# Summing the squares for a norm from a token-major copy of x, and moving the first key projection ahead of it

## The chip, the cores and the metric

The kernel runs on one core of a Trainium2 chip, as one program. The metric is device time in microseconds (us) of one execution. The time of a kernel is the median of its runs. Beside the timed runs there is one execution with the hardware profiler on, and all rows of a trace come from that one.

The core has five engines that work side by side and wait for one another through semaphores: PE (matrix products; PEld is its weight load), DVE (vector operations), ACT (functions, scaled copies), POOL (slower vector work) and SP (which here only issues DMA transfers). Each engine runs its instructions strictly in the order in which they stand.

## The reference, cut to what matters

One step of a hybrid decoder layer: 512 prompt tokens and 8 x 4 sample tokens, 544 rows of 1024 numbers, go through an RMS norm, one wide projection (75 tiles of 128 columns), three token mixers, a merge and an output projection. The change touches only the beginning:

```python
def rmsnorm(x, g):
    xf = x.astype(jnp.float32)
    y = xf * lax.rsqrt(jnp.mean(xf * xf, axis=-1, keepdims=True) + EPS)
    return (y * g.astype(jnp.float32)).astype(x.dtype)
...
parts = split_cols(rmsnorm(x, lp['norm_g']) @ lp['w_in'])
q = rmsnorm(parts['a_q'].reshape(B, T, A_HEADS, A_HD), lp['a_qn']) * (A_HD ** -0.5)
kv = parts['a_kv'].reshape(B, T, 3, 2, A_KV, A_HD)
```

## The kernel before, in words

x is held transposed: `xT` has the 1024 features on 128 partitions in 8 pieces, and the 544 tokens along each row. Every product is made in three parts of reduced-precision operands: a weight tile is split into a rounded part `wh` (ACT, L396) and a rest `wl` (DVE or POOL, L399), the activations into `uh` (ACT, L446) and `ul` (DVE, L449), and PE adds wh·uh, wh·ul and wl·uh over the 8 pieces. One tile is 2 halves of 272 tokens x 24 products (L410, in `gemm_steps`); a half goes into one of two PSUM buffers `pj`, and a sink empties it.

The norm is not applied before the first projections. `uh` and `ul` hold x times the norm's gain only; the factor of each token, 1/sqrt(mean square), is multiplied in when a half is emptied: the sinks at L746 (queries and keys), L755 (values) and L500 (the gate tile) multiply by `rb`, a tile in which the factor of every token stands in all 128 partitions. `rb` is the "row" in question. Nothing that passes through a sink can leave PSUM before `rb` is there.

How `rb` is made before: x is squared piece by piece (POOL L443, ACT L444), pairs of pieces are added (DVE L447), and PE sums over the partitions by products with a column of ones (L453, 4 groups of 5 products, each of which PE runs in two passes, so that the trace counts 10). DVE scales the sums (L460, L461), POOL raises them to -0.5 (L463), PE spreads the 5 columns over all partitions (L468, 10 in the trace), and ACT (L469) and DVE (L470) copy them to `rb`. The sums are interleaved with the 48 products of the first tile (`misc`, the gates; L458), and 13 products of zeros (L438) run ahead of it all. Then come six key and value tiles and four query tiles, on `uh` and `ul`, each with its weight split, its sinks, and for keys and queries a square on ACT (L747) and sums on PE (L742). In the same stretch DVE makes the normalized x for the later tiles (`norm`, L475, L478) and a long series of small gate computations (L609 to L700).

The program is written in one sequence; a scheduler of the framework orders it per engine by its own estimate of times and by priorities. The loads of all weight tiles are issued by SP, in order, into three buffers `wr`; a load waits until the `wl` of the tile three before has been made. Every DMA also waits for the one issued eight before it from SP and ACT together.

Of the kernel before, what the change touches and what calls it, by code (L numbers as in the profile page):

```python
# [19 lines left out]
D = 1024  # L20
T = 512
# [18 lines left out]
NWARM = 13  # L40
# [132 lines left out]
def _layout(i):  # L173
# [4 lines left out]
    d['xT'] = x.T.reshape(8, 128, N).transpose(1, 0, 2)  # L178
    cols = np.array(_col_order())
# [67 lines left out]
def tile_step(ctx: ExitStack, tc: tile.TileContext, A, O):  # L247
# [117 lines left out]
    sqr_ = BS.ring(5, N)  # L365
# [68 lines left out]
    nc.sync.dma_start(out=cst[:, 128:], in_=A['cst'][:, 128:])  # L434
# [4 lines left out]
    pss = pat()  # L439
    pm = [pat()[:, :HF] for h in range(2)]  # L440
    for k in range(0, 8, 2):
        s0, s1 = sqr_(), sqr_()
        nc.gpsimd.tensor_tensor(out=s1, in0=xT[:, k + 1, :], in1=xT[:, k + 1, :], op=ALU.mult)  # L443
        nc.scalar.activation(out=s0, in_=xT[:, k, :], func=AF.Square)  # L444
        for i in (k, k + 1):
            nc.scalar.activation(out=uh[:, i, :], in_=xT[:, i, :], func=AF.Copy, scale=V(VG + i))  # L446
        nc.vector.tensor_tensor(out=s1, in0=s1, in1=s0, op=ALU.add)  # L447
        for i in (k, k + 1):
            nc.vector.scalar_tensor_tensor(out=ul[:, i, :], in0=xT[:, i, :], scalar=V(VG + i), in1=uh[:, i, :].bitcast(F32),  # L449
                                           op0=ALU.mult, op1=ALU.subtract)  # L450
        for i in (0, 1, 2, 4, 3):
            r = 128 if i < 4 else NS
            nc.tensor.matmul(pss[:r, i:i + 1], lhsT=s1[:, i * 128:i * 128 + r], rhs=ones, start=(k == 0 and i == 0),  # L453
                             stop=(k == 6 and i == 3))
        for c in (k, k + 1):
            for j, (w, m) in enumerate(((wt0[0], uh), (wt0[1], uh), (wt0[0], ul))):
                for h in range(2):
                    nc.tensor.matmul(pm[h], lhsT=w[:, c, :], rhs=m[:, c, h * HF:h * HF + HF], start=(c == 0 and j == 0),  # L458
                                     stop=(c == 7 and j == 2))
    nc.vector.tensor_scalar(out=ss[:, :4], in0=pss[:, :4], scalar1=1.0 / D, scalar2=EPS, op0=ALU.mult, op1=ALU.add)  # L460
    nc.vector.tensor_scalar(out=ss[:NS, 4:5], in0=pss[:NS, 4:5], scalar1=1.0 / D, scalar2=EPS, op0=ALU.mult, op1=ALU.add)  # L461
# [7 lines left out]
    nc.scalar.copy(out=rb[:, :T], in_=pb)  # L469
    nc.vector.tensor_copy(out=rb[:, T:], in_=pb2[:, :NS])  # L470
# [17 lines left out]
    nc.vector.tensor_copy(out=ptf, in_=pti)  # L488
    for q in range(NQ):
        nc.vector.tensor_scalar(out=idxf[:, :, q], in0=ptf, scalar1=float(8 * NQ), scalar2=C('pm8'), op0=ALU.mult, op1=ALU.add)  # L490
        nc.vector.tensor_scalar(out=idxf[:, :, q], in0=idxf[:, :, q], scalar1=float(q), scalar2=None, op0=ALU.add)
    nc.vector.tensor_copy(out=idxi, in_=idxf)
# [258 lines left out]
    for b in range(3):  # L751
        rw = rwr()
        raw.append(rw)
        proj(J_KV + 2 * b, qk_sink(b, rw, sqr()))
        proj(J_KV + 2 * b + 1, lambda s, p, b=b: nc.vector.tensor_tensor(out=vTt[b][:, s], in0=p, in1=rb[:, s], op=ALU.mult))  # L755
        with low(400):
            norm(2 * b)
            norm(2 * b + 1)
        nc.scalar.dma_start(out=O['kv'][2 * b + 1], in_=vTt[b])
# [93 lines left out]
    for src, d in ((RBt.rearrange("p b r -> p (b r)"), rb2), (V(VREL, 8), vr2)):  # L853
        nc.scalar.copy(out=d[:, 0, :], in_=src)
        nc.vector.tensor_tensor(out=d[:, 1, :], in0=src, in1=d[:, 0, :].bitcast(F32), op=ALU.subtract)
# [1157 lines left out]
```

## Time and profile before

| | us |
|---|---|
| median of 3 runs | 987.78 |
| lowest and highest of the runs | 981.44, 989.70 |
| the profiled execution | 992.92 |
| its span, first to last instruction | 990.7 |
| PE busy in the span | 940.4 |
| DVE busy in the span | 507.8 |
| ACT, POOL busy in the span | 359.1, 310.0 |

The span is the time from the first to the last instruction; 2.2 us of the profiled execution lie around it. A busy PE is not a PE at its peak: a product counts as busy whether PE's clock is granted at full (2.4 GHz, shown as 1.00) or at half (1.2 GHz, shown as 0.50). Over the span the granted clock is 0.971 on average. Shares over the whole span say little about a change in the first 100 us; the rows that count are those of that stretch.

### The profile page before, as it was taken

The numbers are of one execution on the slowest core, as the hardware profiler recorded it, in microseconds if no ns is written. First come the engines' busy times: TensorE is split into PE (matmuls) and PEld (weight loads), VectorE is DVE, ScalarE is ACT, GpSimd is POOL, SyncE is SP. The second block draws the span as 40 slices with busy tenths as digits, with TensorE's granted clock in tenths as the row PEclk, the third lists the DMA queues.
The fourth block names the chain that finished last, engine by engine and source line by source line (L and its number), as shares of the span: only waits on it lengthen the run. The fifth ranks groups of instructions, "written<-read, shape, count | busy, mean of one in ns | idle before, by whom it ended". The sixth has DMA issues, their size and how long they took to land.

```text
span 990.7 us, 21616 instructions
## 1 busy us (share of the span) xinstructions
PE 940.4 (95%) x8609; PEld 854.9 (86%) x8609; DVE 507.8 (51%) x1256; ACT 359.1 (36%) x728; POOL 310.0 (31%) x369
## 2 busy tenths in 40 slices
PE   8999899799999999999999979999999899999998
PEld 7888798786789977789998959999989777899998
DVE  6895522141122421245775669996585246564622
ACT  4433263232233342324444337665532212232410
POOL 3122522335003471113414332112224213338610
PEclk7999899798999999999999999999999799999999
DMA  5223758556787566788545433125534223375642
GB/s 219 69 82 114 270 170 249 207 164 216 229 283 263 170 216 208 263 267 271 152 136 174 134 105 108 63 73 175 175 121 125 91 89 104 108 225 174 197 165 68
DMA packets 107078, 165.70 MB, mean 167 GB/s; under 512 B 17045, under 2 KB 65430, under 8 KB 106594
## 3 DMA queue, kind: packets, MB, share of 16 engines
q1 hardware_dynamic: 86602, 126.16, 40.3%
q0 software_dynamic: 6752, 22.19, 6.5%
q10 hardware_dynamic: 13624, 15.98, 4.7%
q8 instruction: 68, 1.11, 0.5%
q14 instruction: 32, 0.26, 0.1%
HBM read 139.05 MB, written 33.10 MB: 174 GB/s over the span
## 4 chain that ended last, share of the span: by engine, by line
PE 77%; DVE 10%; DMA 7%; issue 2%; SPq 2%; ACT 1%; another core or an unknown queue 0%; POOL 0%; ACTq 0%; DVEq 0%
PE pj L410 48%; PE pa L354 3%; PE cacc L971 2%; PE pa L1092 2%; PE pacc L1310 2%; PE pg L354 2%; PE pa L983 1%; PE pa L1685 1%; PE pa L1057 1%; PE pa L458 1%; PE pa L1288 1%; PE pa L1286 1%; DMA arena<-in_ps_dram 1%; PE pa L1803 1%; DVE low L1629 1%
## 5 line engine op out<-in xcount | busy, mean ns | idle before, releaser
L410 PE MATMUL pj<-xh,wh 128*128 128x272 f32 x1328 | 215.6, 294 | 4.6 <-DVE arena L1921 1.5
L410 PE MATMUL pj<-xh,wl 128*128 128x272 f32 x1328 | 218.1, 295 | 0.5 <-issue 0.4
L410 PE MATMUL pj<-xl,wh 128*128 128x272 f32 x1328 | 214.3, 293 | 0.2 <-POOL xl L1912 0.2
L410 PEld LDWEIGHTS pj<-xh,wl 128*128 128x128 f32 x1328 | 185.4, 191 | 14.3 <-issue 13.1
L410 PEld LDWEIGHTS pj<-xh,wh 128*128 128x128 f32 x1328 | 183.4, 189 | 15.8 <-issue 10.1
L410 PEld LDWEIGHTS pj<-xl,wh 128*128 128x128 f32 x1328 | 184.0, 190 | 9.0 <-issue 7.3
L396 ACT CAST wh<-wr 128x1024 fp32r<-128x1024 f32 (+1 forms) x107 | 101.9, 953 | 153.0 <-PE pj L410 112.3
L399 POOL TENSOR_TENSOR wl<-wr,wh 128x1024 fp32r<-128x1024 f32 (+1 forms) x34 | 73.3, 2157 | 196.8 <-ACT wh L396 131.8
L399 DVE TENSOR_TENSOR wl<-wr,wh 128x1024 fp32r<-128x1024 f32 (+1 forms) x73 | 83.0, 1137 | 38.2 <-ACT wh L396 16.6
L958 POOL DMA_INDIRECT low<-in_kc_dram,idxi x32 | 30.6, 957 | 48.4 <-PE pa L354 33.2
L1296 ACT ACTIVATE arena<-arena 128x128 f32<-128x128 f32 (+3 forms) x64 | 36.0, 562 | 25.6 <-DVE arena L1295 24.2
L958 POOL DMA_INDIRECT low<-in_vc_dram,idxi x32 | 32.1, 1005 | 33.2 <-PE pa L1057 18.3
L996 DVE COPY arena<-pa 128x512 f32<-128x512 f32 x16 | 11.0, 692 | 56.8 <-PE pa L354 56.8
L354 PE MATMUL pa<-cst,arena 128*128 128x128 f32 (+3 forms) x195 | 31.7, 274 | 5.0 <-issue 1.5
L570 ACT ACTIVATE arena<-pj 128x272 f32<-128x272 f32 x48 | 19.0, 396 | 41.3 <-PE pj L410 36.8
L1298 DVE TENSOR_SCALAR arena<-arena,gat 128x128 f32<-128x128 f32 (+3 forms) x64 | 33.7, 534 | 0.6
L971 PE MATMUL cacc<-arena 128*128 128x64 f32 x256 | 33.8, 277 | 0.0
L971 PEld LDWEIGHTS cacc<-arena 128*128 128x128 f32 x256 | 33.1, 201 | 0.0
L1293 DVE CUSTOM_DVE_ANT_0 arena<-pa,arena 128x128 f32<-128x128 f32 (+3 forms) x64 | 30.5, 483 | 3.3 <-PE pa L1288 2.1
L410 PE MATMUL pj<-uh,wh 128*128 128x272 f32 x160 | 26.7, 304 | 5.2 <-DVE arena L755 4.1
L1523 DVE SCALAR_TENSOR_TENSOR arena<-arena,vec 128x568 f32<-128x568 f32 x36 | 29.7, 826 | 2.3 <-ACT arena L1521 2.1
L410 PEld LDWEIGHTS pj<-uh,wh 128*128 128x128 f32 x160 | 22.5, 196 | 7.8 <-DVE arena L755 4.7
(505 smaller groups left out, 1525.3 us busy)
## 6 DMA issues: line engine op xcount, KB each, us to landing
wr<-in_wt_dram SPq DMA_DIRECT2D x75, 512.0 KB
gq<-in_ps_dram SPq DMA_DIRECT2D x64, 128.0 KB
arena<-in_ps_dram SPq DMA_DIRECT2D x64, 128.0 KB
mgd<-arena ACTq DMA_DIRECT2D x24, 272.0 KB
wr<-in_wb_dram SPq DMA_DIRECT2D x24, 256.0 KB
arena<-mgd SPq DMA_DIRECT2D x16, 272.0 KB
arena<-in_wkT_dram SPq DMA_DIRECT2D x16, 256.0 KB
wr<-in_wo_dram SPq DMA_DIRECT2D x8, 512.0 KB
```

The source lines that it names most:

```text
L354: nc.tensor.transpose(out, in_, ident[:k, :k])
L396: nc.scalar.copy(out=wh[:, :k, :], in_=wr[:, :k, :])
L399: e.tensor_tensor(out=wl[:, :k, :], in0=wr[:, :k, :], in1=wh[:, :k, :].bitcast(F32), op=ALU.subtract)
L410: nc.tensor.matmul(p, lhsT=w[:, c, :], rhs=m[:, (c + rot) % 8, s], start=(i == 0), stop=(i == 3 * k - 1))
L958: nc.gpsimd.indirect_dma_start(out=t.rearrange("p s d -> p (s d)"), out_offset=None, in_=A[src], in_offset=bass.IndirectOffsetOnAxis(ap=id ...
L971: nc.tensor.matmul(acc[:, b * 64:b * 64 + 64].rearrange("p (m x) -> p m x", m=2), lhsT=ks[:, b, :], rhs=qw[:, s::SQ, b, :], start=(q == 0 ...
L1092: nc.tensor.matmul(pw[b * 32:b * 32 + 32], lhsT=QB[:, S * 4 + b, :], rhs=keys[b], start=True, stop=True)
L1293: nc.vector.tensor_tensor_reduce(out=P_[:, :w], in0=ps[g][:, :w], in1=tb[g][:, 512 - w:], scale=1.0, scalar=-3e38, op0=ALU.add, op1=ALU.ma ...
L1296: nc.scalar.activation(out=P_[:, :w], in_=P_[:, :w], func=AF.Exp, bias=st[:, 1:2], accum_out=st[:, 2:3])
L1298: nc.vector.tensor_scalar(out=P_[:, :w], in0=P_[:, :w], scalar1=st[:, 3:4], scalar2=gat[:, i, (g * 4 + r) * 3 + b:(g * 4 + r) * 3 + b + 1] ...
L1310: nc.tensor.matmul(acc[Gh(g), qs], lhsT=vtm[b][:, k, Gh(g)], rhs=pts[b, g][:, k, :], start=(b == 2 and k == 0), stop=False)
L1523: nc.vector.scalar_tensor_tensor(out=cv[:, :568], in0=rw[:, j:j + 568], scalar=cvw[:, t, j:j + 1], in1=cv[:, :568], op0=ALU.mult, op1=ALU.add)
```

## The change

The host lays out x a second time, as it stands, one token per row (`xn`, 544 x 1024 numbers). It is loaded in five loads, tokens on the partitions, and each row is squared and summed by one instruction: on ACT for loads 0, 2 and 4, on DVE for loads 1 and 3. The squares, the pairwise sums and PE's products with ones go. The first key tile's 48 products are written ahead of the norm; its two halves stay in PSUM until `rb` is there, and its sinks run then. The load of the larger part of the constants moves behind the first key tile's weights. There are 20 zero products ahead and three pairs more, written between the pieces. Within the gate tile, a piece's products with `ul` and `wl` now follow the next piece's products with `uh`. Some small operations (`issue_after`) are held until `rb` has been copied.

```diff
-NWARM = 13
+NWARM = 20
...
+    d['xn'] = x
...
-    nc.sync.dma_start(out=cst[:, 128:], in_=A['cst'][:, 128:])
...
-        nc.gpsimd.tensor_tensor(out=s1, in0=xT[:, k + 1, :], in1=xT[:, k + 1, :], op=ALU.mult)
-        nc.scalar.activation(out=s0, in_=xT[:, k, :], func=AF.Square)
...
-        nc.vector.tensor_tensor(out=s1, in0=s1, in1=s0, op=ALU.add)
...
-            nc.tensor.matmul(pss[:r, i:i + 1], lhsT=s1[:, i * 128:i * 128 + r], rhs=ones, start=(k == 0 and i == 0),
-                             stop=(k == 6 and i == 3))
...
+        misc(k, [(wt0[0], uh)])
+        if k:
+            misc(k - 2, [(wt0[0], ul), (wt0[1], uh)])
+        if k < 6:
+            for i in range(2):
+                nc.tensor.matmul(pz, lhsT=hl_[:, 0, :128], rhs=hl_[:, 0, :512], start=True, stop=True)
+    misc(6, [(wt0[0], ul), (wt0[1], uh)])
+
+    kv0 = []
+    gemm(wload(A['wt'][J_KV], 8), uh, ul, 8, lambda s, p: kv0.append((s, p)))
+    nc.sync.dma_start(out=cst[:, 128:], in_=A['cst'][:, 128:])
+
+    XN = Reg(5 * D, True)
+    for i in range(5):
+        r = 128 if i < 4 else NS
+        xn = XN.t(D)[:r]
+        nc.sync.dma_start(out=xn, in_=A['xn'][i * 128:i * 128 + r, :])
+        if i % 2:
+            with tc.issue_after(uls.ins):
+                nc.vector.tensor_tensor_reduce(out=xn, in0=xn, in1=xn, scale=1.0, scalar=0.0, op0=ALU.mult, op1=ALU.add,
+                                               accum_out=ss[:r, i:i + 1])
+        else:
+            nc.scalar.activation(out=xn, in_=xn, func=AF.Square, accum_out=ss[:r, i:i + 1])
+    XN.free()
...
-        proj(J_KV + 2 * b, qk_sink(b, rw, sqr()))
+        if b:
+            proj(J_KV + 2 * b, qk_sink(b, rw, sqr()))
+        else:
+            sink = qk_sink(b, rw, sqr())
+            for s, p in kv0:
+                sink(s, p)
```

PE, the beginning of the program. `hl` holds the zeros, `pa_121` to `pa_123` and `pa_127`, `pa_128` are PSUM buffers for the sums and the gate tile, `wh_99` and `wl_100` that tile's weights. Before:

```order
L438 MATMUL pa_107<-hl 128x512 x13
L453 MATMUL pa_121<-ones,arena 128x1 x3
L453 MATMUL pa_121<-ones,arena 32x1
L453 MATMUL pa_121<-ones,arena 128x1
L458 MATMUL pa_122<-uh,wh_99 128x272
L458 MATMUL pa_123<-uh,wh_99 128x272
L458 MATMUL pa_122<-uh,wl_100 128x272
```

Of the change, in the same place:

```order
L437 MATMUL pa_106<-hl 128x512 x20
L457 MATMUL pa_106<-hl 128x512 x6
L444 MATMUL pa_127<-uh,wh_99 128x272
L444 MATMUL pa_128<-uh,wh_99 128x272
L444 MATMUL pa_127<-uh,wh_99 128x272
```

The sums are gone, and the six further zero products (L457) stand ahead of the first piece and not between the pieces.

PE, from the end of the gate tile to the spreading of the factors (`pj_393`, `pj_422` before, `pj_205`, `pj_230` after are the two halves of the first key tile). Before:

```order
L458 MATMUL pa_122<-ul,wh_99 128x272
L458 MATMUL pa_123<-ul,wh_99 128x272
L410 MATMUL pj_393<-uh,wh_389 128x272 x8
L410 MATMUL pj_393<-ul,wh_389 128x272 x8
L410 MATMUL pj_393<-uh,wl_390 128x272 x8
L410 MATMUL pj_422<-uh,wh_389 128x272
L468 MATMUL pa_224<-cst,rstd 128x128 x4
L468 MATMUL pa_225<-cst,rstd 128x32
```

Of the change:

```order
L410 MATMUL pj_205<-uh,wh_201 128x272 x8
L410 MATMUL pj_205<-ul,wh_201 128x272 x8
L410 MATMUL pj_205<-uh,wl_202 128x272 x8
L410 MATMUL pj_230<-uh,wh_201 128x272 x8
L410 MATMUL pj_230<-ul,wh_201 128x272 x8
L410 MATMUL pj_230<-uh,wl_202 128x272 x8
L483 MATMUL pa_269<-cst,rstd 128x128 x4
L483 MATMUL pa_270<-cst,rstd 128x32
```

Before, 25 products of the first key tile stand ahead of the spreading; now all 48 do.

DVE, around the copy of its part of `rb` (L470 before, L485 after). Before:

```order
L399 TENSOR_TENSOR wl_390<-wr_387,wh_389 128x1024
L491 TENSOR_SCALAR arena<-arena 128x8 x4
L460 TENSOR_SCALAR ss<-pa_121 128x4
L461 TENSOR_SCALAR ss<-pa_121 32x1
L492 CAST idxi<-arena 128x32
L399 TENSOR_TENSOR wl_454<-wr_451,wh_453 128x1024
L470 COPY arena<-pa_225 128x32
L500 TENSOR_TENSOR arena<-pa_122,arena 128x272
```

Of the change:

```order
L471 ISA arena,ss<-arena 128x1024
L471 ISA ss 128x1
L476 TENSOR_SCALAR ss<-ss 128x5
L399 TENSOR_TENSOR wl_443<-wr_440,wh_442 128x1024
L399 TENSOR_TENSOR wl_508<-wr_505,wh_507 128x1024
L485 COPY arena<-pa_270 128x32
L504 CAST arena<-pti 128x8
L516 TENSOR_TENSOR arena<-pa_127,arena 128x272
```

The rests of the second and the third weight tile after the gates (`wl_443`, `wl_508`) stand ahead of the copy now, where only the second's did before, and the ten small operations on page indices (the kind of L488 to L492) stand behind it.

## Rows read from the trace of the kernel before

**Rows 1.** The chain of waits, first 130 us: start us, us, what.

```profile
11.20 4.90 PE pa L458 x20
16.11 1.11 PE pa L453 x10
...
25.35 3.66 PE pj L410 x25
29.01 0.91 PE pa L468 x8
29.94 0.60 ACT arena L469
30.56 0.79 DVE arena L500 x2
...
105.71 3.47 another core or an unknown queue
```

**Rows 2.** The page's part 4, the chain's shares of the whole span.

```profile
PE 77%; DVE 10%; DMA 7%; issue 2%; SPq 2%; ACT 1%; another core or an unknown queue 0%; POOL 0%; ACTq 0%; DVEq 0%
```

**Rows 3.** Busy by stretch: PE, PEld, DVE, ACT, POOL, PE clock, DMA share, GB/s.

```profile
5.00:14.00 9.00, 7.04 (x31) 5.95 (x31) 7.29 (x11) 8.41 (x15) 5.28 (x4) 0.74 1.03 412
14.00:15.00 1.00, 1.00 (x7) 1.00 (x6) 1.00 (x2) 1.00 (x2) 1.00 (x2) 0.50 0.68 270
...
30.27:50.00 19.73, 17.95 (x130) 16.83 (x131) 19.31 (x30) 9.01 (x16) 4.83 (x3) 0.92 0.20 70
50.00:81.34 31.34, 28.03 (x215) 25.75 (x214) 29.79 (x47) 9.72 (x16) 9.24 (x6) 1.00 0.26 87
```

**Rows 4.** The same view in stretches of one granted clock.

```profile
9.30:16.10 6.80, 6.16 (x28) 5.83 (x26) 6.80 (x7) 5.79 (x9) 4.96 (x4) 0.50 0.82 324
16.10:19.50 3.40, 3.40 (x31) 3.34 (x30) 3.40 (x11) 0.00 (x0) 0.00 (x0) 0.99 0.00 0
19.50:26.30 6.80, 6.80 (x34) 6.77 (x33) 1.82 (x9) 0.91 (x1) 1.20 (x1) 0.50 0.24 80
26.30:46.90 20.60, 18.82 (x147) 17.54 (x147) 17.50 (x26) 8.58 (x15) 4.83 (x3) 1.00 0.16 53
```

**Rows 5.** PE in order of time: start us, us, line, operation, idle before.

```profile
2.07 5.01 PE L438 MATMUL pa<-hl 128*128 128x512 f32 x13 [2.07 <-DVE hl L374]
8.40 1.50 PE L453 MATMUL pa<-ones,arena 128*128 128x1 f32 x10 [1.32 <-DVE arena L447]
...
12.73 0.66 PE L458 MATMUL pa<-uh,wl 128*128 128x272 f32 x2
13.18 0.66 PE L458 MATMUL pa<-ul,wh 128*128 128x272 f32 x2
...
31.15 1.16 PE L410 MATMUL pj<-ul,wh 128*128 128x272 f32 x8
32.15 1.16 PE L410 MATMUL pj<-uh,wl 128*128 128x272 f32 x8
```

**Rows 6.** Groups by line: busy us, mean ns, idle before (first row: ns min/median/max).

```profile
L1600 ACT ACTIVATE low<-low x1: 1064/1064/1064, 679.5 to 679.5; 128x1024 f32<-128x1024 f32 x1
...
L399 DVE TENSOR_TENSOR wl<-wr,wh 128x1024 fp32r<-128x1024 f32 x9 | 11.0, 1217 | 3.4 <-ACT wh L396 3.3
L1293 DVE CUSTOM_DVE_ANT_0 arena<-pa,arena 128x512 f32<-128x512 f32 x16 | 10.9, 684 | 2.0 <-PE pa L1288 1.5
L463 POOL TENSOR_TENSOR rstd<-ss,mhalf 128x5 f32<-128x5 f32 x1 | 1.2, 1197 | 7.8 <-DVE idxi L492 7.8
```

**Rows 7.** DVE in order of time, columns as in rows 5.

```profile
6.93 0.79 DVE L449 SCALAR_TENSOR_TENSOR ul<-arena,vec,uh 128x544 fp32r<-128x544 f32 x1 [1.65 <-ACT uh L446]
...
19.09 0.49 DVE L490 TENSOR_SCALAR arena<-arena,cst 128x8 f32<-128x8 f32 x3
...
80.20 0.68 DVE L669 TENSOR_TENSOR arena<-sm,arena 4x512 f32<-4x512 f32 x1
80.90 0.44 DVE L746 TENSOR_TENSOR arena<-pj,arena 128x272 f32<-128x272 f32 x1
```

More of the change, by code (lines that the diff above doesn't have):

```diff
@@ L364, in tile_step @@
     xT, xnr, rb = X.t(8, N), X.ring(2, N), X.t(N)
-    sqr_ = BS.ring(5, N)
     xh = rp.tile([128, 8, N], R32, tag="xh", name="xh")
@@ L438, in tile_step, with misc @@
         nc.tensor.matmul(pz, lhsT=hl_[:, 0, :128], rhs=hl_[:, 0, :512], start=True, stop=True)
-    pss = pat()
     pm = [pat()[:, :HF] for h in range(2)]
+    def misc(k, ops):
+        for c in (k, k + 1):
+            for w, m in ops:
+                for h in range(2):
+                    nc.tensor.matmul(pm[h], lhsT=w[:, c, :], rhs=m[:, c, h * HF:h * HF + HF], start=(c == 0 and w is wt0[0] and m is uh),
+                                     stop=(c == 7 and w is wt0[1]))
     for k in range(0, 8, 2):
-        s0, s1 = sqr_(), sqr_()
-        nc.gpsimd.tensor_tensor(out=s1, in0=xT[:, k + 1, :], in1=xT[:, k + 1, :], op=ALU.mult)
-        nc.scalar.activation(out=s0, in_=xT[:, k, :], func=AF.Square)
@@ L445, in tile_step @@
         for i in (k, k + 1):
             nc.scalar.activation(out=uh[:, i, :], in_=xT[:, i, :], func=AF.Copy, scale=V(VG + i))
-        nc.vector.tensor_tensor(out=s1, in0=s1, in1=s0, op=ALU.add)
         for i in (k, k + 1):
[L449 to L452, printed above, removed]
-            nc.tensor.matmul(pss[:r, i:i + 1], lhsT=s1[:, i * 128:i * 128 + r], rhs=ones, start=(k == 0 and i == 0),
-                             stop=(k == 6 and i == 3))
@@ L455, in tile_step @@
[L455 to L461, printed above, removed]
+            uls = nc.vector.scalar_tensor_tensor(out=ul[:, i, :], in0=xT[:, i, :], scalar=V(VG + i), in1=uh[:, i, :].bitcast(F32),
+                                                 op0=ALU.mult, op1=ALU.subtract)
@@ L462, in tile_step @@
+    XN.free()
+    nc.vector.tensor_scalar(out=ss, in0=ss, scalar1=1.0 / D, scalar2=EPS, op0=ALU.mult, op1=ALU.add)
     rstd = cpt("rstd", [128, 5])
@@ L468, in tile_step @@
         nc.tensor.matmul(o, lhsT=rstd[:r, i:i + 1].to_broadcast([r, 128]), rhs=ident[:r, :r], start=True, stop=True)
-    nc.scalar.copy(out=rb[:, :T], in_=pb)
-    nc.vector.tensor_copy(out=rb[:, T:], in_=pb2[:, :NS])
+    rba = nc.scalar.copy(out=rb[:, :T], in_=pb)
+    rbs = nc.vector.tensor_copy(out=rb[:, T:], in_=pb2[:, :NS])
     def norm(k):
@@ L487, in tile_step @@
     nc.sync.dma_start(out=pti, in_=A['pt'])
[L488 to L492, printed above, removed]
+    with tc.issue_after(rbs.ins):
+        nc.vector.tensor_copy(out=ptf, in_=pti)
+        for q in range(NQ):
+            nc.vector.tensor_scalar(out=idxf[:, :, q], in0=ptf, scalar1=float(8 * NQ), scalar2=C('pm8'), op0=ALU.mult, op1=ALU.add)
+            nc.vector.tensor_scalar(out=idxf[:, :, q], in0=idxf[:, :, q], scalar1=float(q), scalar2=None, op0=ALU.add)
+        nc.vector.tensor_copy(out=idxi, in_=idxf)
     ID.free()
@@ L853, in tile_step @@
     for src, d in ((RBt.rearrange("p b r -> p (b r)"), rb2), (V(VREL, 8), vr2)):
-        nc.scalar.copy(out=d[:, 0, :], in_=src)
-        nc.vector.tensor_tensor(out=d[:, 1, :], in0=src, in1=d[:, 0, :].bitcast(F32), op=ALU.subtract)
+        with tc.issue_after(rba.ins):
+            nc.scalar.copy(out=d[:, 0, :], in_=src)
+        with tc.issue_after(rbs.ins):
+            nc.vector.tensor_tensor(out=d[:, 1, :], in0=src, in1=d[:, 0, :].bitcast(F32), op=ALU.subtract)
     for k in range(2):
```

## The prediction

> **What bounds the kernel now.** I read the page's chain shares first, then the chain of waits over the first 130 us, then busy time by stretch, and last the instructions of PE and DVE in that stretch. The chain is PE's for 77% of the span [rows 2], so a gain made early is worth something only if it moves the time at which PE's later work can start, and the rest of the program then follows it.
>
> The beginning is a chain of its own. PE works on the gate tile and the sums from 11.2 us, goes straight on into 25 products of the first key tile, and spreads the norm's factors only at 29.0; ACT copies them into `rb` at 29.94 to 30.54, and the first operation that uses `rb` starts on DVE at 30.56 [rows 1]. From there DVE is the bound: it is busy 19.31 of 19.73 us and 29.79 of 31.34 us up to 81.34 [rows 3], where it has emptied the 13th of the 20 halves of the key, value and query tiles (it starts that at 80.90) [rows 7]. Only then is PE free to run on: it waits for DVE inside that stretch, and the remaining halves follow at its own pace. So two things matter: when `rb` is there, and how much DVE has to do between `rb` and the 13th half.
>
> Why PE is late with `rb` is in the clock. From 9.30 to 16.10 the granted clock is 0.50, the half level (1.2 GHz), then 0.99 to 19.50, then 0.50 again to 26.30, and 1.00 after that [rows 4]. Ahead of the first fall PE had been idle for 1.32 us and had run one group of sums [rows 5]; ahead of the second it was busy all the time, but with sums among the gate products (1.11 us of sums stand on the chain at 16.11 [rows 1]). At half, two gate products start every 0.45 us (12.73 to 13.18), 0.226 each; at full, eight start every 1.00 us (31.15 to 32.15), 0.125 each [rows 5].
>
> **The change part by part.** All times are from the span's start. The profiled execution took 992.92, 5.1 above the median of 987.78; I work out a difference on the trace and take it from the median.
>
> PE up to the spreading. The 13 zero products take 5.01 us from 2.07 [rows 5]. Now 26 stand in a row, since the order puts the six "between the pieces" ahead of the first piece. In that respect the change does not do what it says; PE is kept busy ahead of the pieces instead. No row has 26. Upper bound for their end: all at the mean of the 13 (0.385), 2.07 + 26 x 0.385 = 12.1. Lower: the second 13 at full, 512/272 x 0.125 = 0.235 each, 2.07 + 5.01 + 13 x 0.235 = 10.1. I take 10.1, since nothing interrupts them. Then 48 gate and 48 key products follow with no sums in between: 96 x 0.125 = 12.0 at full, 96 x 0.226 = 21.7 at half. I take full: dense products of this size ran at 1.00 from 26.30 to 46.90 [rows 4], and the two things that stood ahead of the falls, the idle time at 7 us and the sums, are gone. End at 22.1. The spreading takes 0.91 and ACT's copy 0.60 [rows 1]: `rb` at 23.6.
>
> Is the data there? The first `ul` starts at 6.93 and takes 0.79 [rows 7]; with the pair sums gone from DVE, eight of them and one weight rest (1.22 [rows 6]) need 7.5 us, so the last is there at 14.5. PE needs it near its 40th gate product, at 10.1 + 5.0 = 15.1. No wait worth counting; if it is 1 us late, `rb` is 1 us late.
>
> The sums of squares. DMA moves 412 GB/s at a share of 1.03 from 5 to 14 us and is done by about 14.9 (share 0.68 in the last of these us) [rows 3]; by then x, the constants and four weight tiles have landed. The copy adds 544 x 4096 bytes = 2.23 MB, 5.4 us at 412. It stands on SP ahead of the second and third weight tile after the gates' (0.52 MB each, 2.5 us together). So those end at 14.9 + 5.4 = 20.3 and the copy at 17.8. ACT squares and sums 1024 columns in 1.06 (by the row of L1600, the same shape), DVE in 2 x 0.68 = 1.37 (by the 512-column row of L1293, the same instruction) [rows 6]. The last on either is done near 19.2, the factor on POOL (1.20 [rows 6]) near 20.6, ahead of PE's 22.1 by 1.5 us. So the removed work is replaced by work that is hidden by PE; if PE were ready at once, this path would set `rb` at 22.1.
>
> A new queue on DVE. The rest `wl_508` stands ahead of DVE's copy into `rb`. Its tile lands at 20.3; ACT's cast (taken as the 1.06 of L1600, same columns) and the rest (1.22) end it at 22.6, ahead of `rb` by 1.0 us. Behind it wait the copy, all sinks, and so PE's next tile. It costs nothing as long as the loads keep their rate.
>
> The Trainium skill speaks against that rate: "DMA: Bandwidth & Descriptors", section Bandwidth, asks for transfers of at least 1 MiB for 75% of the peak, and these are of half that size; with the 341 GB/s it lists for 1 MB, the copy would take 6.5 us by that page, and `wl_508` would be ready about 0.1 us after `rb`. The trace does not agree: loads of 0.5 MB ran together at 412 [rows 3].
>
> So DVE's `rb` work starts at 23.6 instead of 30.56: 7.0 us earlier.
>
> DVE from there to the 13th half. Before: 80.90 - 30.56 = 50.3 us. One weight rest fewer lies in it (1.22 [rows 6]). The order puts the 13th sink ahead of two operations of the size of L669 (0.68 [rows 7]), which it followed: 1.4 less. Ten small index operations come in, at 0.16 (three take 0.49 [rows 7]): 1.6 more; one other small one that moved in is below 1.06. Sum: 1.0 us less; bounds, 2.6 less (the small ones in gaps) to 0.5 more. I take 1.0.
>
> PE's own state costs nothing there: the first key tile holds both `pj` buffers until `rb` comes, so PE idles from the end of the spreading to the first sink, some 2 us, and may fall to half for a while. It had 25 of 48 products of that tile done at `rb` before and has all now, so DVE stays the bound.
>
> Sum: 7.0 + 1.0 = 8.0 us less at the 13th half. Six halves of PE's work follow, unchanged, and the later order is the same but for a few neighbours that swap. I carry it to the end: 987.78 - 8.0 = 979.8 (984.9 against the profiled execution).
>
> **The rivals.**
>
> 1. PE falls to, or stays at, the half level. For it: it did so twice in this stretch, once while busy without a pause [rows 4]. Against it: sums and the pause are gone. If zeros end at 12.1 and all 96 products run at half, PE is done at 33.8, and with a spreading of twice 0.91 and the copy `rb` comes at 36.2, 5.6 later than before; less 1.0 on DVE, the kernel is slower by 4.6: 992.4. It decides from about 7.0 + 1.0 = 8.0 us of loss, that is from 79 products at half (0.101 each).
>
> 2. The copy of x comes late. For it: 2.23 MB more in a stretch where DMA is at its limit [rows 3], and weights behind it. If it moves at half of 412, it needs 10.8 us; `wl_508` is then done at 22.6 + 5.4 = 28.0, 4.4 after the forecast's `rb`, and 8.0 - 4.4 = 3.6 are left: 984.2. Against it: the rows of the load are no smaller than those of `xT`.
>
> 3. Part of the gain is lost behind the projections. At 105.71 the chain waits 3.47 us for something the trace does not name [rows 1]; if this wait ends when it did, or one like it comes at another place, 8.0 - 3.5 = 4.5 are left: 983.3.
>
> 4. More is gained: the unnamed wait of 3.47 falls away and DVE's stretch is 1.6 shorter (its lower bound): 8.0 + 5.1 = 13.1, 974.7.
>
> **How the numbers follow.** The forecast holds 0.54, with its own range of 976 to 984 (`rb` 1.5 us either way, DVE's bounds, some 2 us in later waits); rival 1 has 0.06, rival 2 0.11, rival 3 0.12, rival 4 0.17. The runs of before spread by 8 us themselves, so each case is spread by some 3. The range from 969 to 987 leaves out most of rival 1 and the ends of 2, 3 and 4, in all about 0.2. About what can be told from no change is 1%, 9.9 us: faster than that is below 977.9. Rival 4 gives 0.15 to it, the forecast 0.19 of its 0.54, and the spread of 2 and 3 some 0.04: 0.38. Slower than 997.7 needs rival 1 and a bad spread, or something I do not see: 0.05. Within: 0.57.
>
> **What would show it.** Right: a granted clock of 1.00 from about 6 us to the end of the first key tile, no half level at 10 to 26; the gate tile's products over by about 16 us and the first key tile's by 22; `rb` copied at 23 to 24; the 13th sink at 72 to 74; DVE near fully busy in between. Wrong: 0.50 in the listing between 10 and 22 (rival 1); ACT's squares waiting for DMA past 20 us, or DVE's `wl_508` after the spreading (rival 2); an early 13th sink but no earlier start of the later tiles (rival 3). If `rb` is early and the 13th sink is not, my account of DVE's queue is wrong.

## The result, and the profile after

The changed kernel took 974.15 us (median of 8 runs, 970.25 to 978.85) against 988.09 for the kernel before (8 runs, 977.68 to 992.55): 13.9 us less. The ratio, which leaves out runs in the chip's slower state, is 0.9883 (95% interval 0.9841 to 0.9925), 11.6 us less. The profiled execution has a span of 971.5 us and a mean granted clock of 0.982 (before: 990.7 and 0.971). Two later series of runs (a series is what was timed together on one chip), each with the kernel before among them, gave 0.9954 (0.9927 to 0.9981) and 0.9922 (0.9890 to 0.9954), that is 4.5 and 7.7 us less; the three ratios together come to about 8. The gain is clear of noise in each series, but it is about 1% of the time and so below the 2% from which a kernel is called faster here.

Busy time by stretch in the changed kernel, with the columns of [rows 3], which the first, fourth and fifth row answer, and in the last three rows by the clock, as in [rows 4]:

```profile
5.00:14.00 9.00, 9.00 (x53) 8.02 (x53) 7.04 (x10) 8.19 (x12) 0.27 (x1) 1.00 1.02 412
14.00:16.00 2.00, 2.00 (x18) 2.00 (x18) 1.47 (x2) 1.15 (x2) 0.00 (x0) 1.00 1.04 414
16.00:20.00 4.00, 4.00 (x34) 4.00 (x33) 1.97 (x4) 2.03 (x3) 0.00 (x0) 1.00 1.05 344
24.96:50.00 25.04, 20.47 (x148) 19.05 (x149) 23.44 (x43) 10.68 (x18) 8.91 (x5) 0.93 0.27 85
50.00:73.77 23.77, 22.18 (x174) 20.71 (x172) 22.83 (x39) 6.49 (x10) 4.66 (x4) 1.00 0.28 91
...
8.60:26.49 17.89, 15.39 (x118) 14.95 (x117) 13.08 (x23) 11.79 (x20) 1.46 (x2) 1.00 0.89 321
26.49:29.90 3.41, 3.41 (x18) 3.41 (x17) 3.41 (x12) 2.46 (x5) 1.38 (x1) 0.50 0.38 136
29.90:50.00 20.10, 16.47 (x130) 15.02 (x130) 18.50 (x27) 7.16 (x11) 7.53 (x4) 1.00 0.22 67
```

The granted clock is 1.00 until 26.49, where [rows 4] have 13.6 us of 0.50 in two pieces. One stretch has to be left out of that: the column prints 1.00 also ahead of the first clock record of a trace, and there the products tell. Of the zero products, 9 fit into the 3.7 us from 2.30 on and 12 into the 2.5 us from 6.00 on, so PE ran at half until about 6 us and at full from there:

```profile
2.30:6.00 3.70, 3.70 (x9) 2.91 (x10) 0.21 (x2) 1.30 (x2) 0.00 (x0) 1.00 0.99 367
6.00:8.50 2.50, 2.50 (x12) 2.01 (x11) 1.54 (x3) 2.50 (x5) 0.00 (x0) 1.00 1.02 418
```

The half level from 26.49 to 29.90 comes behind `rb`, at first while PE waits for DVE anyway. DVE stays the bound from `rb` on: 46.27 of 48.81 us busy. DMA moves 412 to 414 GB/s until 16 us, then 344.

The same kernel in order of time, columns as in [rows 5] and [rows 7], engines mixed:

```profile
2.07 6.68 PE L437 MATMUL pa<-hl 128*128 128x512 f32 x20 [2.07 <-DVE ss L380]
8.59 1.53 PE L457 MATMUL pa<-hl 128*128 128x512 f32 x6
9.96 1.17 PE L444 MATMUL pa<-uh,wh 128*128 128x272 f32 x8
...
15.97 1.17 PE L410 MATMUL pj<-uh,wh 128*128 128x272 f32 x8
...
19.12 1.06 ACT L474 ACTIVATE arena<-arena 32x1024 f32<-32x1024 f32 x1 [1.30 <-DMA arena<-in_xn_dram]
20.56 1.20 POOL L478 TENSOR_TENSOR rstd<-ss,mhalf 128x5 f32<-128x5 f32 x1 [7.34 <-DVE ss L476]
22.00 1.39 PE L483 MATMUL pa<-cst,rstd 128*128 128x128 f32 x10
22.57 1.04 ACT L396 CAST wh<-wr 128x1024 fp32r<-128x1024 f32 x1 [1.21 <-DMA wr<-in_wt_dram]
23.53 0.58 ACT L484 COPY arena<-pa 128x512 f32<-128x512 f32 x1
23.65 1.23 DVE L399 TENSOR_TENSOR wl<-wr,wh 128x1024 fp32r<-128x1024 f32 x1 [1.02 <-ACT wh L396]
24.96 0.43 DVE L516 TENSOR_TENSOR arena<-pa,arena 128x272 f32<-128x272 f32 x1
25.89 1.64 PE L410 MATMUL pj<-uh,wh 128*128 128x272 f32 x8 [2.50 <-DVE rv L878]
...
73.77 0.44 DVE L762 TENSOR_TENSOR arena<-pj,arena 128x272 f32<-128x272 f32 x1
```

PE goes from zeros to gate tile to key tile to spreading without a pause, and spreads at 22.00 instead of 29.01 [rows 1]. ACT's copy into `rb` ends at 24.11, but the first use (L516) stands on DVE behind the weight rest `wl_508` (L399 at 23.65), whose load ACT awaited until 22.57: 24.96, against 30.56 before. The 13th half is emptied from 73.77 on, 80.90 before [rows 7], 7.1 earlier.

That is 7 of the 19.2 us by which the two profiled spans differ. Comparing the starts of the same instructions, some 5 more come at 98 to 122 us and about 9 between 160 and 240 (some 3 up to 203, some 5 between 217 and 236). What of that belongs to the change is the question of the experiments.

### The profile page after: what moved, and what is told of

It reads as the page before. It is cut to its first block, busy times and chain, and to the rows that moved or that the text cites. A ratio compares the mean times of both kernels' runs of the same rounds, so it can differ in the third digit from the quotient of the medians.

```text
span 971.5 us, 21569 instructions
## 1 busy us (share of the span) xinstructions
PE 928.9 (96%) x8582; PEld 844.3 (87%) x8582; DVE 504.7 (52%) x1255; ACT 360.7 (37%) x730; POOL 304.5 (31%) x365
## 5 line engine op out<-in xcount | busy, mean ns | idle before, releaser
L410 PEld LDWEIGHTS pj<-xh,wl 128*128 128x128 f32 x1328 | 183.7, 189 | 13.6 <-issue 12.4
L399 POOL TENSOR_TENSOR wl<-wr,wh 128x1024 fp32r<-128x1024 f32 (+1 forms) x34 | 72.9, 2144 | 191.2 <-ACT wh L396 127.3
L399 DVE TENSOR_TENSOR wl<-wr,wh 128x1024 fp32r<-128x1024 f32 (+1 forms) x73 | 84.3, 1155 | 39.3 <-ACT wh L396 18.1
```

Of the source, the lines that this page charges most:

```text
L399: e.tensor_tensor(out=wl[:, :k, :], in0=wr[:, :k, :], in1=wh[:, :k, :].bitcast(F32), op=ALU.subtract)
L410: nc.tensor.matmul(p, lhsT=w[:, c, :], rhs=m[:, (c + rot) % 8, s], start=(i == 0), stop=(i == 3 * k - 1))
```

## The experiments

Theory 1: the change gains by the time at which `rb` is there, and the program follows that one to one; what the profiles show beyond it is not the change's. Theory 2: the earlier `rb` also takes later waits away. Theory 3, formed after the second series: the changed schedule has a gain of its own near 160 us. Several kernels alter single instructions after scheduling, so that the order on every engine stays exactly as it was, except for what the diff says.

All in one table: us at half clock between the zeros and the spreading; first use of `rb`; start of the 13th and of the 20th sink; PE's wait near 160 to 187 us for the sixth block of `wkT`; the median; the ratio to before in the same series. In late8 and late24 the half level falls into PE's wait for POOL; that of thin_zeros is read from its products, see there.

| kernel | half | `rb` | 13th | 20th | wait | median | ratio (95%) |
|---|---|---|---|---|---|---|---|
| before, first profile | 13.6 | 30.56 | 80.90 | 103.09 | 6.33 | 988.09 | 1 |
| changed, first profile | 0 | 24.96 | 73.77 | 95.89 | 3.21 | 974.15 | 0.9883 (0.9841 to 0.9925) |
| late8 | 2.4 | 30.23 | 79.62 | 101.79 | 4.26 | 987.89 | 0.9976 (0.9941 to 1.0011) |
| late24 | 12.4 | 42.98 | 92.43 | 114.56 | 3.52 | 999.53 | 1.0103 (1.0051 to 1.0156) |
| thin_zeros | 5.6 | 25.89 | 75.16 | 97.33 | 3.63 | 983.05 | 0.9908 (0.9873 to 0.9942) |
| more_zeros | 3.4 | 26.66 | 77.03 | 99.20 | 8.72 | 990.00 | 0.9987 (0.9953 to 1.0021) |
| after_again | 0 | 25.02 | 74.05 | 96.22 | 3.41 | 977.28 | 0.9954 (0.9927 to 0.9981) |
| before_again | 3.4 | 26.17 | 75.89 | 98.07 | 6.66 | 988.94 (one run) | none |
| key_behind | 0.3 | 24.83 | 77.60 | 99.77 | 4.50 | 979.82 | 0.9971 (0.9943 to 0.9999) |
| key_first_only | 0 | 27.64 | 75.70 | 98.75 | 5.64 | 986.31 | 1.0013 (0.9975 to 1.0052) |
| before_wkT_ahead | 20.5 | 33.29 | 83.02 | 106.07 | 6.64 | 983.15 | 0.9970 (0.9935 to 1.0006) |
| after_wr_ahead | 0 | 24.78 | 74.17 | 96.28 | 6.49 | 980.51 | 0.9947 (0.9924 to 0.9970) |
| after_wkT_early | 0 | 24.62 | 72.43 | 94.60 | 1.78 | 973.97 | 0.9880 (0.9842 to 0.9919) |
| after_third | 0 | 24.50 | 72.23 | 94.40 | 3.41 | 977.22 | 0.9922 (0.9890 to 0.9954) |

The median of before was 993.08 in the series of the four kernels from late8 to more_zeros, 982.79 in the next (to key_first_only), 985.72 in the last, so only kernels of one series are compared by their times. Each profile from late8 on is of a run of its series.

### The same kernel with a later `rb`

POOL's raising works on 8 or 24 copies of the five columns. With late8:

```diff
-    rstd = cpt("rstd", [128, 5])
+    rstd = cpt("rstd", [128, 40])[:, :5]
...
+    new = copy.replace(POW.ins, outs=[copy.replace(POW.ins.outs[0], ap=[o[0], [5, 8], o[1]])],
+                       ins=[copy.replace(x, ap=[list(x.ap[0]), [0, 8], list(x.ap[1])]) for x in POW.ins.ins])
```

> The changed kernel with every instruction in the same order, but POOL's raising to -0.5 works on 40 columns instead of 5 (eight copies side by side, of which one is used). It takes longer and so makes `rb` later by some s, which the trace shows; all else is untouched. Theory 1 (`rb` shifts DVE's stretch and the rest follows one to one): the 13th sink starts s later than 73.77, the time is 974.15 + s less the slack of about 1 us that this path has. Theory 2 (the gain beyond 8 us comes with the shift too, as later waits and falls of the clock go away when all is earlier): for s near 5 the time is 974.15 + 10 or more, and a wait that the trace does not name stands near 105 us again. Rival (it isn't `rb` that counts): the time stays at 974 within 3.

> The same with 120 columns. If POOL's time grows with the columns, s is some 10 to 15 us, `rb` is later than it was before the change, and theory 1 gives 974.15 + s less 1, about 984 to 988; theory 2 gives the time of before, 988, or more, with the unnamed wait back. Rival (not `rb`): 974 within 3.

In order of time, late8:

```profile
20.53 6.80 POOL L478 TENSOR_TENSOR rstd<-ss,mhalf 128x40 f32<-128x40 f32 x1 [7.16 <-DVE ss L476]
...
30.23 0.43 DVE L516 TENSOR_TENSOR arena<-pa,arena 128x272 f32<-128x272 f32 x1
```

and late24:

```profile
20.51 19.57 POOL L478 TENSOR_TENSOR rstd<-ss,mhalf 128x120 f32<-128x120 f32 x1 [7.08 <-DVE ss L476]
...
42.98 0.43 DVE L516 TENSOR_TENSOR arena<-pa,arena 128x272 f32<-128x272 f32 x1
```

Within this series three kernels have the identical order: thin_zeros (below), late8 and late24. Their `rb` is used at 25.89, 30.23 and 42.98, their medians are 983.05, 987.89 and 999.53: 4.84 us for a shift of 4.34, and 11.64 for 12.75. One to one, as theory 1 has it, over a range three times as wide as the change's. With `rb` at 30.23, where the first profile of before has it, 2.4 us of the gain are left (interval -1.1 to 5.9). The medians of 6 and 12 runs leave some 3 us of doubt in each difference. The absolute time that was expected (974.15 + s less 1) was not met: late8 is 9.5 above it. Before itself is 5.0 slower in this series, which covers about half of that; the shift was met.

### Zeros

thin_zeros gives the 26 products 16 columns:

```diff
+    few = lambda p: copy.replace(p, ap=[list(p.ap[0]), [1, 16]]) if p.ap[-1][1] == 512 else p
...
+                f.instructions[i] = copy.replace(x, outs=[few(p) for p in x.outs], ins=[few(p) for p in x.ins])
```

> The changed kernel in the same order, but the 26 zero products have 16 columns instead of 512, so PE does next to nothing until the first piece is there at about 8 us. Theory 1 (an idle PE ahead of the gate tile is what brought the half level): the granted clock is 0.50 for a stretch of 6.8 us that begins between 8 and 16, the key tile ends at 25 to 28 instead of 22.0, `rb` is used at 27 to 30 instead of 24.96, and the time is 977 to 980. Rival (the zero products have no part in it, the sums on PE alone brought the half level): the clock is 1.00 throughout, the key tile ends by 22 and the time is 974 within 2.

more_zeros repeats the seventh zero product of the kernel before 13 times:

```diff
+            x = f.instructions[k[6]]
+            for j in range(13):
+                f.instructions.insert(k[6], copy.replace(x, name=nc.get_next_instruction_name(), sync_info=None))
```

> The kernel before in the same order, with 13 more zero products behind the 13 (26 in all, as in the changed kernel); the sums on PE stay. Theory 1: the zeros end at about 10 and take the first half level stretch (9.3 to 16.1) away, but the second (19.5 to 26.3) stays since the sums stay; 6.8 us at half hold 3.4 of work, less 1 for the later start of the first group: `rb` is used 2 to 3 us earlier than 30.56, the time is 985 to 986. Rival A (the zeros are the whole gain): both stretches go, `rb` at about 24 to 25, the time 975 to 982. Rival B (zeros do nothing here): 988 within 2.

thin_zeros, in order of time:

```profile
2.07 4.44 PE L437 MATMUL pa<-hl 128*128 128x16 f32 x20 [2.07 <-DVE ss L380]
```

and busy by stretch:

```profile
9.00:24.00 15.00, 15.00 (x104) 15.00 (x103) 9.94 (x14) 9.30 (x15) 3.19 (x2) 1.00 0.91 331
```

more_zeros, busy by stretch:

```profile
9.00:19.00 10.00, 10.00 (x83) 9.74 (x81) 10.00 (x17) 5.26 (x9) 4.44 (x4) 1.00 0.57 220
19.00:24.00 5.00, 5.00 (x29) 5.00 (x29) 2.64 (x9) 1.05 (x1) 1.20 (x1) 0.66 0.32 105
```

Thin products are no idle PE: each still takes 0.222 us, and PE counts as busy. So this run doesn't test idleness, as it was meant to. It does show a difference to the wide ones. The 1.00 in its row stands partly ahead of the trace's first clock record; the products tell otherwise. Of the gate tile, in order of time:

```profile
8.56 2.18 PE L444 MATMUL pa<-uh,wh 128*128 128x272 f32 x8 [0.77 <-ACT wh L396]
10.54 0.66 PE L444 MATMUL pa<-ul,wh 128*128 128x272 f32 x2
10.99 0.66 PE L444 MATMUL pa<-uh,wl 128*128 128x272 f32 x2
...
15.15 0.41 PE L444 MATMUL pa<-ul,wh 128*128 128x272 f32 x2
15.40 0.41 PE L444 MATMUL pa<-uh,wl 128*128 128x272 f32 x2
```

Two start every 0.45 us, the half level's pace, and from about 14.1 on two every 0.25. So the gate tile ran at half for 5.6 us, where in the changed kernel its first eight take 1.17 us, the pace of full. That costs about 2.8 us (half of 5.6). The tile begins 1.4 earlier, at 8.56 instead of 9.96, and so `rb` is only 0.9 later. The run lies between the two expectations: a stretch at half as theory 1 had it, but the key tile ends at 23.2, not at 25 to 28.

In more_zeros, with the sums still on PE, there is no half level until 19.11 and one of 3.4 us there, as theory 1 said. That the added zeros did it is not shown by one profile, since the unchanged beginning varies as much (next section). `rb` is used at 26.66, but the time is that of before (0.9987, expected 985 to 986 of 988, or 0.997 to 0.998, which the interval includes).

### The two kernels once more, and two parts of the change

after_again, before_again and after_third are the kernels unaltered; of before_again there is a profile and no time of its own. key_behind takes the first key tile back behind the norm:

```diff
-    gemm(wload(A['wt'][J_KV], 8), uh, ul, 8, lambda s, p: kv0.append((s, p)))
...
+        proj(J_KV + 2 * b, qk_sink(b, rw, sqr()))
```

key_first_only puts it ahead in the kernel before, ahead of L460:

```diff
+    kv0 = []; gemm(wload(A['wt'][J_KV], 8), uh, ul, 8, lambda s, p: kv0.append((s, p)))
     nc.vector.tensor_scalar(out=ss[:, :4], in0=pss[:, :4], scalar1=1.0 / D, scalar2=EPS, op0=ALU.mult, op1=ALU.add)
```

> The changed kernel once more, unaltered, timed anew and with a second profile. In the first profile it has no wait at the copy into `gpk` (L740, near 98 us), where the kernel before and the four kernels of the first call all wait 3.4 to 3.5 us for something the trace does not name, and no half level between 105 and 125 us. Theory 1 (that wait is not set by the time of `rb`; it comes in some executions and not in others): the wait is there in this profile, the end of the query tiles is at 98 to 99 as before, and the profiled span is some 5 to 10 us longer than 971.5; the ratio to before stays near 0.988 to 0.992. Theory 2 (the earlier `rb` takes the wait away): no such wait again, the span within 2 us of 971.5 but for the chip, ratio near 0.986 to 0.988.

> The kernel before, unaltered, with a second profile. Both theories expect the half level at 9.3 and 19.5 us and `rb` used at 30.5; theory 2 the unnamed wait at `gpk` near 105.7 again; theory 1 leaves open whether it is there.

> The changed kernel with the first key tile traced where it was before, behind the norm: PE spreads the factors right behind the gate tile and the 48 products come after it. The sums (copy of x, ACT, DVE, POOL) end at about 21.8, so PE idles from 16 to 22 and `rb` is used at 24 to 25 as in the changed kernel. Theory 1 (DVE is the bound from `rb` on, and the key tile ahead only fills PE's wait): PE has the 48 products still to do, the first key sink comes at about 30 instead of 25.3, but DVE has the gate's sinks, the norm and the small operations meanwhile; the 13th sink is at 74 to 76 and the ratio to before is 0.988 to 0.992. Rival (the 6 us of products moved ahead of the wait are a gain of their own): the 13th sink at 78 to 80 and the ratio 0.993 to 0.996.

> The kernel before with one part of the change alone: all 48 products of the first key tile stand ahead of the spreading (before: 25). The sums stay on PE, 13 zero products. Theory 1: 23 more products stand on the way to `rb`, 2.9 us at full clock to 5.2 at half, so `rb` is used at 33.5 to 36 and the ratio is 1.002 to 1.005, less what DVE finds done. Rival (the first key tile ahead is where the gain comes from): the ratio is 0.99 to 0.995.

Busy by stretch (9 to 22 and 22 to 30 us), PE's clock in the third number from the right. before_again:

```profile
9.00:22.00 13.00, 11.85 (x86) 11.54 (x87) 11.81 (x24) 6.15 (x10) 6.04 (x5) 0.87 0.46 175
22.00:30.00 8.00, 8.00 (x65) 7.84 (x65) 5.18 (x10) 4.45 (x8) 0.00 (x0) 1.00 0.35 126
```

before_wkT_ahead, which is the kernel before up to 160 us:

```profile
9.00:22.00 13.00, 11.84 (x55) 11.57 (x55) 11.29 (x21) 5.35 (x9) 4.53 (x4) 0.53 0.48 179
22.00:30.00 8.00, 8.00 (x39) 7.97 (x38) 1.53 (x4) 1.05 (x1) 1.20 (x1) 0.50 0.12 49
```

key_first_only:

```profile
9.00:29.00 20.00, 17.24 (x138) 16.73 (x138) 15.66 (x31) 9.07 (x15) 5.88 (x5) 1.00 0.47 170
```

after_third:

```profile
9.00:22.00 13.00, 13.00 (x99) 12.68 (x98) 9.33 (x14) 8.77 (x15) 1.56 (x2) 1.00 1.01 380
```

Here is what the first pair of profiles could not tell. The beginning of the kernel before is the same program in before, before_again and before_wkT_ahead, and its clock stood at half for 13.6, 3.4 and 20.5 us, so `rb` was used at 30.56, 26.17 and 33.29. The expectation of half levels at 9.3 and 19.5 in before_again was wrong: one of 3.4 us at 10.24 was all. Three profiles of the changed kernel and four of its variants with the same zeros (late8, late24, after_wr_ahead, after_wkT_early) have none in the gate and key tile, and the five in which nothing holds `rb` back use it at 24.50 to 25.02. key_first_only had none either, with the sums and the pauses still there: these do not always bring it. Its `rb` came at 27.64, not at 33.5 to 36 as expected.

At full clock the kernel before would hardly be later at `rb` than the changed one, by an estimate from two spreadings:

```profile
24.46 1.39 PE L468 MATMUL pa<-cst,rstd 128*128 128x128 f32 x10
25.93 1.39 PE L469 MATMUL pa<-cst,rstd 128*128 128x128 f32 x10
```

The first, of before_again, less the 1.7 us that 3.4 us at half cost, gives 22.8; `rb` is used 1.71 after the spreading: 24.5. The second, of key_first_only, has 23 more products, 2.9 us, ahead: 23.0, and `rb` at 24.7. So at `rb` the change gains about what the clock would have cost and no more: three groups of sums go (1.05 us each at full in key_first_only), and 23 products of 0.125 come ahead. This makes the gain differ with the execution of the kernel before. Whether it is why one series gives 11.6 us and another 4.5 is not shown, as the timed runs have no traces. What they do have is the mean granted clock of each run, and it varies: over the 26 runs of before in the last series from 0.966 to 0.984, and the time falls as it rises (correlation -0.84); over the 9 of after_third from 0.974 to 0.982. In which stretch the clock was lost, these figures do not say.

The extra gain near 100 us in the first pair does not go by the kernel. In order of time, the copy into `gpk`, in after_again:

```profile
98.75 0.27 DVE L740 COPY gpk<-pa 64x64 f32<-64x64 f32 x1 [0.76 <-PE pa L736]
```

and in late8:

```profile
107.81 0.28 DVE L740 COPY gpk<-pa 64x64 f32<-64x64 f32 x1 [3.43 <-remote]
```

This wait of 3.4 to 3.5 us is in the first profile of before and in all four kernels of late8's series, of either order; it is in none of the eight profiles of the two other series, of either order, nor in the first of the changed kernel. So the program does not decide on it; the series and its chip may, which no run separates. In the same five traces, and in no other, such unnamed waits stand again near 220 us, here in before:

```profile
225.50 0.69 DVE L1065 COPY arena<-pa 128x512 f32<-128x512 f32 x1 [7.55 <-remote]
```

That is where the first pair gains its 5 us between 217 and 236, and the two other pairs of profiles gain nothing there. So a good part of what the first two spans differ by is not the change's. Of theory 2 that leaves nothing here. Theory 1 had expected the wait in after_again, where it did not come; its reading, that the wait comes and goes by itself, holds.

key_behind has `rb` at 24.83, but its 13th sink is 3.6 later than after_again's, and its 20th, too: PE has 48 products to do when DVE could begin. PE had waited 4.05 us for POOL's factors before, and its clock was at half from 20.0 to 26.8:

```profile
20.31 2.64 PE L483 MATMUL pa<-cst,rstd 128*128 128x128 f32 x10 [4.05 <-POOL rstd L478]
```

The 13th sink lies between what theory 1 and the rival expected, the ratio above both, as does after_again's; before has its lowest median in this series. The time is 2.5 us above after_again's (979.82, 977.28), which is not clear of noise. By the two profiles, moving the key tile ahead is worth some 3.5 us of PE's time that DVE does not fill; up to 3.3 of it can be the half level, which began in that wait. key_first_only, the same move without the rest, shows no change (1.0013, 0.9975 to 1.0052).

### The place of one load near 160 us

Between 150 and 200 us the starts in before_again fall another 4 us behind those in after_again, and a step of 3 to 4 us stands in the other pairs. There PE waits for the sixth block of `wkT`: 5.6 to 8.7 us in before's order, 3.2 to 4.5 in the changed one. On SP, before has the load of a weight tile (`wr`) ahead of it, the changed schedule has it behind, which nothing in the change asks for. Three kernels move that one load, here before_wkT_ahead:

```diff
-L393 DMA wr<-in_wt_dram 128x1024
-L978 DMA arena<-in_wkT_dram 128x512 x3
+L978 DMA arena<-in_wkT_dram 128x512
+L393 DMA wr<-in_wt_dram 128x1024
+L978 DMA arena<-in_wkT_dram 128x512 x2
```

after_wr_ahead is the opposite swap in the changed kernel, and after_wkT_early takes the block six `in_ps` loads further ahead.

> The kernel before with two neighbouring loads on SP swapped, near 162 us: the sixth block of `wkT` ahead of the weight tile's load `wr`, as the changed kernel happens to have them; nothing else moves. In the traces of before's order PE waits 5.6 to 8.7 us for that block (L983), in those of the change's order 3.4 to 4.5. Theory 3 (beside `rb`, the change gains some 3 us because its schedule put that load ahead): the wait is 2 to 4 us shorter than in before's order and the ratio to before is 0.996 to 0.998. Rival (the wait goes by how early everything is, or by the traffic, not by this order): the wait stays at 6 to 9 us and the ratio is 1.000 within 0.002.

> The changed kernel with the opposite swap: the weight tile's load ahead of the sixth block of `wkT`, as before. Theory 3: PE's wait at L1006 near 160 us grows from 3.4 to 6 or 7, and the kernel is 2 to 4 us slower than the changed one in the same call. Rival: the wait is 3 to 4.5 as it was, and the time that of the changed kernel within 1.5.

> The changed kernel with that block of `wkT` issued six `in_ps` loads earlier on SP (0.62 us each, some 3.7 us). Theory 3 (this wait is on the path): PE's wait of 3.4 us at L1006 shrinks to 0 to 1 us and the half level of 10.2 us that begins in it (163 us) may go too; the kernel is 2 to 6 us faster than the changed one, a ratio to before of 0.985 to 0.993. Rival (another load ends as late, or SP waits for the block's buffer and holds up the `in_ps` loads): no gain, within 1.5 us of the changed kernel.

> The changed kernel unaltered, on the same chip as the three above, for comparison. From the two earlier ratios (0.988 and 0.995): theory 1 with theory 3 (what `rb` gains here depends on how long before's clock fell, 1 to 6 us, plus some 3 us later) gives 0.988 to 0.996.

In order of time, SPq being the issue, after_third:

```profile
157.14 0.34 SPq L1001 DMA_DIRECT2D arena<-in_wkT_dram  x1
...
161.93 1.97 PE L1006 MATMUL pa<-arena 128*128 128x64 f32 x8 [3.41 <-DMA arena<-in_wkT_dram]
```

after_wr_ahead:

```profile
160.11 1.44 SPq L1001 DMA_DIRECT2D arena<-in_wkT_dram  x3
...
166.85 1.97 PE L1006 MATMUL pa<-arena 128*128 128x64 f32 x8 [6.49 <-DMA arena<-in_wkT_dram]
```

after_wkT_early:

```profile
157.48 0.34 SPq L1001 DMA_DIRECT2D arena<-in_wkT_dram  x1
...
160.70 1.19 PE L1006 MATMUL pa<-arena 128*128 128x64 f32 x8 [1.78 <-DMA arena<-in_wkT_dram]
```

and what its SP waited for between 140 and 170 us (total, times, longest):

```profile
SPq L1001 <- DMA arena<-in_ps_dram: 6.3, 2, 5.0
```

before_wkT_ahead:

```profile
170.99 0.34 SPq L978 DMA_DIRECT2D arena<-in_wkT_dram  x1
...
177.32 1.97 PE L983 MATMUL pa<-arena 128*128 128x64 f32 x8 [6.64 <-DMA arena<-in_wkT_dram]
```

In the changed order theory 3 holds both ways. With `wr` ahead the wait is 3.1 longer and the time 3.3 (980.51, 977.22); with the block further ahead the wait is 1.6 shorter, the half level behind it 3.4 us instead of 10.2, and the time 3.25 less (973.97). The block was not issued earlier in that kernel, though: SP had to wait 5.0 us for an older `in_ps` load to land and issued it at 157.48. It arrived sooner because six loads stood behind it instead of ahead (3.2 us from issue to PE's start, 4.8 in after_third). In before's order the swap alone did not shorten the wait (6.64); the ratio is where theory 3 had it (0.9970), but it cannot be told from 1 (0.9935 to 1.0006), and without a shorter wait it does not speak for the theory. So the short wait of the changed kernel belongs to its order and this load's place in it, but the place alone doesn't carry over; why SP issues it so late in before's order was not tried further.

The median of after_wkT_early is below those of both kernels: 973.97 against 977.22 and 985.72 in the same series. The wait was expected to shrink to 0 to 1 us, and 1.78 was left.

## Why the prediction was right, and where not

The forecast was 979.8, 8.0 less than before. The first measurement showed 13.9 less by the medians and 11.6 by the ratio, the three together about 8; the mechanism is the forecast one, and the sizes are off in places.

- PE ahead of the spreading. Zeros to 10.1, gate and key tile to 22.1 at full clock: 9.96 and 22.00. Rival 1, the half level, came in none of the seven profiles of the changed order with its wide zeros. The reasons given against that rival do not carry far: the pause and the sums, whose absence was to keep the clock up, stand in key_first_only, and it ran at full.
- The path of the sums. Forecast ready at 20.6 with 1.5 us in hand; POOL was done at 21.76, with 0.24 in hand. The loads set that: the copy of x was awaited until 19.12, not 17.8.
- The queue on DVE. This step failed: `wl_508` was to be done at 22.6, 1.0 ahead of `rb`; it was done at 24.88, 0.77 behind ACT's copy, as its load was awaited until 22.57. So `rb` was used at 24.96, not 23.6, 5.6 us earlier than before and not 7.0. Rival 2 is right in kind and small in size (the rows of this load are a little smaller than those of xT's, 4096 bytes against 4352, not "no smaller"). (In after_third ACT's copy into `rb` ends at 24.46 and `wl_508` at 24.30, so there the queue did not decide.) Since DVE is the bound and would have had to make this rest later, little should be lost by it; no run shows that.
- Why the loads were late. The bytes moved as forecast: 347 GB/s on average up to 20.30 us are 7.04 MB, and x, its copy, the constants and the four weight tiles that the prediction counts are 7.1. What it left out is the load of the next weight tile, issued on SP at 16.72, when its buffer had come free. Up to 22.57 us 7.63 MB had moved, which is all that and this tile of 0.52 MB. The copy of x shared DMA in the same way with the tile issued behind it: it and all ahead of it are 6.04 MB, and 6.56 had moved by 19.12. So loads in flight together ended late together, and not one after another at the full rate as the sum has it.

```profile
16.72 0.33 SPq L393 DMA_DIRECT2D wr<-in_wt_dram  x1
...
0.00:20.30 20.30, 18.23 (x109) 16.67 (x110) 11.78 (x21) 11.96 (x18) 1.87 (x13) 1.00 0.92 347
0.00:22.57 22.57, 20.50 (x128) 18.94 (x129) 13.12 (x23) 13.01 (x19) 3.07 (x14) 1.00 0.90 338
```

- The Trainium skill's page "DMA: Bandwidth & Descriptors", section Bandwidth, with 341 GB/s for loads of 1 MB, would have put the end of the copy at 18.9, an estimate; the trace has 19.12. That these are near is chance: up to 16 us the trace has 412 to 414 GB/s, and the copy was late because other loads ran beside it.
- DVE from `rb` to the 13th half: 48.81 against 50.3, 1.5 less, forecast 1.0. (The bound of 0.5 more does not follow from its terms, which give 0.1 more.) Over three profiles of either beginning it is 48.5 against 49.9.
- Sum at the 13th half: 7.1 earlier, forecast 8.0.
- "I carry it to the end": right in that a shift is carried one to one (late8, late24). The later order, however, was not "the same but for a few neighbours that swap" in its effect: one such neighbour, the load on SP, is worth 3.3 us in the changed kernel. This term was missing.
- Rival 4, "the unnamed wait falls away": it did in the first pair, but not by the change, since the wait comes and goes with either program. That the first median, 974.15, is so near this rival's 974.7 is luck. Rival 3's wait is the same one.
- The size of 7.0 rested on one execution of the kernel before. By three profiles `rb` is used there at 30.0 on average, 5.2 later than in the three of the changed kernel (24.8), with a range of 7.1 against 0.5. 5.2, 1.4 and 3.1 (the wait: 6.5 in two profiles of before, 3.3 in three after) make 9.7, near the 8 or so of the three series. The profiles lean one way, though: the three executions of before's beginning took 5 to 6 us more than the medians of their kernels, those of the changed kernel 1 to 2 less.
- So that the forecast's 8.0 and the measured 8 or so agree is in part luck: the term for `rb` was some 1.8 too large, that for DVE 0.4 too small, and the 3 us of the load were not in the sum.

What stays open: why the granted clock falls in the beginning of the kernel before in one execution for 3.4 us and in another for 20.5; that the sums on PE bring it is not shown, since key_first_only has them and ran at full. What the unnamed waits wait for. What the later order is worth beyond that one load. Whether less to load ahead of `wl_508` would pay was not tried.

## What to carry to other kernels

Where the stretch to be shortened contains a fall of the clock, take a second and a third profile of the unchanged kernel before sizing the gain: the price of that stretch is then a range. Here the change gained about the average of it and a steadier beginning. Read the clock of the first microseconds from the pace of the products, since a clock column may print 1.00 where the trace has no record. Count every load that is in flight beside the one you wait for, not only those issued ahead of it. Move a term by itself, with the order held fixed, to see that it is carried to the end, and look at what the scheduler reshuffled far behind the edit: the place of one load among others on SP was worth as much as a stage of the edit, and could be moved for 3 us more.

## What the runs showed of the hardware that was not expected

- The same instructions in the same order had a granted clock of 0.50 for 3.4, 13.6 and 20.5 us ahead of the spreading in three executions.
- 20 zero products of 16 columns, each with a weight load of its own, took 4.44 us, 0.222 each, and 20 of 512 columns 6.68. With 26 thin ones ahead PE kept the pace of the half level until about 14.1 us, with 26 wide ones until about 6.
- Loads issued one behind the other ended late together: with a weight tile's load issued 2.5 us behind it, the one awaited came at 22.57 us, although as many bytes as stood up to it had moved by about 20.4.
- POOL's raising to a power costs by the column: 1.20 us for 5, 6.80 for 40, 19.57 for 120, some 0.16 for each.
- SP stood 5.0 us ahead of one issue, waiting for an older load to land (after_wkT_early).
